# One 512-column matmul for two of 256 in the FFN's first product

## The chip, the core and the metric

The kernel runs on one core of a Trainium2 chip. The metric is the time of one execution in microseconds (us), and of several executions the median. Engines are named as the profile names them: PE is the matmul engine and PEld its weight loads, DVE the vector engine, ACT the scalar engine, POOL the GpSimd engine, SP the engine that issues most transfers. In a matmul the stationary operand is a weight load of 128x128 numbers, and the moving operand is streamed past it, 256 or 512 columns at a time.

## The reference, cut to what matters

A decoder block on 256 tokens of 2048 channels in fp32: two kinds of attention, a merge, and then the part that is changed, a gated MLP with a causal convolution of three taps. `D_FF` is 5632.

```python
    h2 = rmsnorm(x, ffn_norm_w[l])
    up = causal_dwconv(h2 @ w_ffn_up[l], conv_w[l], conv_b[l])
    a, b = jnp.split(up, 2, axis=-1)
    x = x + (jax.nn.silu(a) * b) @ w_ffn_down[l]
return rmsnorm(x, final_norm_w)
```

## The kernel before

All weights of the block are streamed once, in the order of use, in halves of a megabyte (128 partitions of 1024 numbers, 512 KB). Each number is split into a high and a low part that the matmul engine takes exactly (`split2`): ACT copies the high part (`whi`, L129), DVE subtracts it from the number (`wlo`, L130). The activations are split in the same way (`xh`, `xl` for the second norm's output). A product is then three matmuls: high by high, high by low, low by high; low by low is left out. `mm3` records these three.

The work goes in slots, one for each megabyte of weights, 252 in all. In a slot the kernel splits the two halves of the next slot (`part`), lets each task of the postprocessing take one stage (`run_tasks`), and then issues this slot's products (`products`, `issue`). All engines take their instructions in the order of the code. There are four buffers of a split half (`PART_BUFS`), so ACT can start on a half when PE has finished the half that lay there four halves earlier.

A group is 512 columns of one weight matrix. The FFN's first product (kind `up`) has 22 groups of four slots, n = 0, 2, .. 42. A group holds four blocks of 128 columns: of channel blocks n and n+1 the part that becomes `a` and the part that becomes `b`. Its weights are stationary and the 256 tokens move, so a slot is four row tiles by four blocks by three matmuls of 256 columns, 48 matmuls, and a group is 192. The four blocks accumulate in the two PSUM banks of `acc`, two blocks in a bank; `acc` has two buffers, four banks. The other four banks belong to small tiles of the attention and of transposes (`att`).

After a group, two tasks `ffn` run beside the next group's products, the second two slots later, each in four stages: the scaled product into `u` (DVE, L469), the convolution in `y` (ACT L474, DVE L477), the gate `g` (ACT L481, DVE L482), and the split of `g` (ACT L129, DVE L130). The last part of the kernel (kind `dn`) has the weights moving in 512 columns and the activations stationary.

Of the kernel before, what the change touches and what calls it, by code (L numbers as in the profile page):

```python
# [29 lines left out]

# columns of the table of per-channel vectors
V_ATTN, V_RET, V_FFN, V_CONV = 0, 16, 24, 40
# [5 lines left out]
def pieces_in():  # L38
    """Column pieces of w_in, in the order in which the kernel uses them."""
    rw, mw = RH * RD, MH * MD  # L40
    rq, rk, rv, rg = 0, rw, 2 * rw, 3 * rw
    mq = 4 * rw
    mk, mv = mq + mw, mq + 2 * mw
    gr = mq + 3 * mw
    gm = gr + D
    out = []
    for hg in range(2):
        out.append(("mv", hg, [(mv + CW * hg, CW)]))
        for hp in range(2):
            h = 4 * hg + 2 * hp  # L50
            out.append(("mqk", h, [(b + MD * x, MD) for x in (h, h + 1) for b in (mk, mq)]))
    for hg in range(2):
        out.append(("rv", hg, [(rv + CW * hg, CW)]))
        out.append(("rg", hg, [(rg + CW * hg, CW)]))
        for h in (2 * hg, 2 * hg + 1):
            out.append(("rqk", h, [(rk + RD * h, RD), (rq + RD * h, RD)]))
    gates = [(("gr", c, [(gr + CW * c, CW)]), ("gm", c, [(gm + CW * c, CW)])) for c in range(D // CW)]
    return out, gates


def plan():
    """Groups of 512 columns: (what, which, weight, columns, rows)."""
    first, gates = pieces_in()
    groups = [(k, n, "w_in", cols, D) for k, n, cols in first]
    for c in range(D // CW):
        for k, n, cols in gates[c]:
            groups.append((k, n, "w_in", cols, D))
        groups.append(("um", c, "w_moba_up", [(CW * c, CW)], MH * MD))
        groups.append(("ur", c, "w_ret_up", [(CW * c, CW)], RH * RD))
    for c in range(D // CW):  # L70
        groups.append(("wo", c, "w_out", [(CW * c, CW)], D))
    for f in range(0, NFB, 2):
        cols = [(b + P * x, P) for x in (f, f + 1) for b in (0, DFF)]
        groups.append(("up", f, "w_ffn_up", cols, D))
    for c in range(D // CW):
        groups.append(("dn", c, "w_ffn_down", [(CW * c, CW)], DFF))
    return groups
# [3 lines left out]
def block(ctx: ExitStack, tc: tile.TileContext, a):  # L81
# [4 lines left out]
    wp = ctx.enter_context(tc.tile_pool(name="wp", bufs=1))  # L86
    ps = ctx.enter_context(tc.tile_pool(name="ps", bufs=1, space=PSUM))
    px = ctx.enter_context(tc.tile_pool(name="px", bufs=1))
    left, right = ExitStack(), ExitStack()
# [7 lines left out]

# [1 line left out]
    raws, parts = {}, {}  # L99
# [14 lines left out]
    def part(n, *some):  # L114
        """Split a half of a megabyte and send for the one that takes its place."""
        if n < n_halves:
            if n not in parts:
                parts[n] = [wp.tile([P, 2 * CW], F32R, name=x, bufs=PART_BUFS) for x in ("whi", "wlo")]
            for w in some or spans(n):
                split2(parts[n][0][:, w], parts[n][1][:, w], raws[n][:, w])  # L120
            if not some or some[0] == spans(n)[-1]:
                raws.pop(n)
                load(n + RAW_BUFS)

# [1 line left out]
    def split2(hi, lo, full, scale=None):  # L126
        """hi + lo = full (times a number by partition), each exact in fp32r."""
        if scale is None:
            nc.scalar.activation(hi, full, AF.Copy)  # L129
            nc.vector.tensor_sub(lo, full, f32(hi))  # L130
        else:
            nc.scalar.activation(hi, full, AF.Copy, scale=scale)  # L132
            nc.vector.scalar_tensor_tensor(lo, full, scale, f32(hi), op0=OP.mult, op1=OP.subtract)  # L133
# [14 lines left out]
    def issue():  # L148
        """The products of the stream; after a third of them, the others in between."""
        n, m = len(stream), len(between)  # L150
        first, done = n // 3, 0
        for i, one_mm in enumerate(stream):
            one_mm()
            while done < m and done * (n - first) < (i + 1 - first) * m:
                between[done]()
                done += 1
        assert done == m
        stream.clear()
        between.clear()

    def att(name):
        return ps.tile([P, 512], F32, name=name, tag="att", bufs=4)

# [6 lines left out]
    def rsqrt(name, ss, n):  # L170
        """(ss / n + EPS) ** -0.5 by token."""
        nt = ss.shape[1]
        ms = sb.tile([P, nt], F32, name=name + "ms", bufs=2)
        nc.vector.tensor_scalar(ms, ss, 1.0 / n, EPS, op0=OP.mult, op1=OP.add)
        r = sb.tile([P, nt], F32, name=name, bufs=2)
        nc.gpsimd.tensor_tensor(r, ms, mhalf[:, :nt], op=OP.pow)
        return r

    def across(r):
        """[P, NT] by token to [P, S], the same in each partition."""  # L180
        t = att("across")
# [3 lines left out]

# [1 line left out]
    tasks = []  # L187
# [23 lines left out]
    nc.gpsimd.memset(mhalf, -0.5)  # L211
    xh = px.tile([P, KD, S], F32R, name="xh")
    xl = px.tile([P, KD, S], F32R, name="xl")
    ot = {k: px.tile([P, 8, S], F32R, name="ot" + k) for k in ("rh", "rl", "mh", "ml")}
# [38 lines left out]
    def setup():  # L253
        """Constants and the first norm."""
        yield
# [43 lines left out]
    def moba(acc, h, vh, vl):  # L299
        """One head from its keys and queries, [d, (k q) tokens] in PSUM."""  # L300
        hv = slice((h % 4) * MD, (h % 4 + 1) * MD)
# [47 lines left out]
    def retention(acc, h, vh, vl, gate):  # L349
        """One head from its keys and queries, [d, (half tokens)] in a bank each."""  # L350
        hv = slice((h % 2) * RD, (h % 2 + 1) * RD)
# [54 lines left out]
    def flipped(full, dsth, dstl, k0, weight):  # L406
        """[tokens, 512] to hi and lo of its transpose, [channel, k0 .., tokens]."""
        trs = []
# [48 lines left out]
    def ffn_slot(f):  # L457
        """Where the FFN's activations of a block lie, hi and lo."""
        if f < 8:
# [5 lines left out]
    def ffn(acc, f):  # L465
        """A pair of blocks, [channel, (a b) tokens] in PSUM."""
        pf = big["pf"]
        u = big["u"][f % 2]
        nc.vector.tensor_mul(u[:, :, 2:], pair(acc), twice(big["r2b"]))  # L469
        yield  # L470
        y = pf.tile([P, 2, S], F32, name="y", bufs=2)
        cv = [vec[:, V_CONV + 4 * (f + j * NFB):V_CONV + 4 * (f + j * NFB) + 4] for j in range(2)]
# [22 lines left out]
    def finish(acc, t):  # L495
        """The last columns of a tile of tokens, its norm and its way out."""
        c = D // CW - 1
# [16 lines left out]

# [1 line left out]
    now = {}  # L516

    def opened(kind, n):
        """The activations that a group's weights meet: hi and lo, [channel, k, tokens]."""
        if kind in ("mv", "rv"):  # L520
# [27 lines left out]

    def closed(kind, n, acc):
        if kind in ("mv", "rv"):  # L550
# [27 lines left out]
        elif kind == "up":  # L578
            if n == 0:
# [5 lines left out]
                for u in big["u"]:  # L585
                    nc.vector.memset(u[:, :, 0:2], 0.0)
            spawn(ffn, acc[:, 0, :], n)
            spawn(ffn, acc[:, 1, :], n + 1, after=2)
        elif kind == "dn" and n < D // CW - 1:
# [15 lines left out]
    def products(kind, act, accs, kc, halves, tokens, nk):  # L605
        """A megabyte of weights (four tiles of rows) with the activations."""
        for h, (hi, lo) in enumerate(halves):
            for j in range(2):
                kt = 4 * kc + 2 * h + j
                begin, end = kt == 0, kt == nk - 1  # L610
                xs = ffn_slot(kt) if kind == "dn" else [x[:, kt, :] for x in act]
                if kind in ("mqk", "rqk", "up"):
                    for b in range(4):
# [11 lines left out]
    for kind, n, _, _, rows in groups:  # L625
        nk = rows // P
        act = opened(kind, n)
        acc = ps.tile([P, 2, 512], F32, name="acc", bufs=2)
        accs = [acc[:, t, :] for t in range(NT)]
        if (kind, n) == groups[-1][:2]:  # L630
            accs[1] = att("acc1")
        for kc in range(nk // 4):
# [16 lines left out]
            slot += 1  # L649
        closed(kind, n, acc)  # L650
    assert not tasks and not between
    right.close()
    left.close()


# [1 line left out]
def stream(inputs):  # L657
    """The weights in the order of use, in tiles of 256 rows by 512 columns: [n, 128, 1024]."""
    out = []
# [7 lines left out]
def constants():  # L667
    """Angles, decays and masks: what depends on shapes alone."""
    f = np.float32
# [53 lines left out]
```

## Time and profile before

| what | value |
|---|---|
| time, median of 3 runs | 1470.79 us (1470.59 to 1471.25) |
| span of the profiled execution, first to last instruction | 1469.1 us |
| median less span | 1.7 us |
| granted PE clock, mean over the span | 0.997 |
| PE busy | 1455.8 us, 99% of the span |
| products of `up`, first to last | 712.4 to 1220.6 us |
| groups n = 2 to 42 of `up` | 736.73 to 1220.57 us |

The profiled execution has no time of its own beside its span; what a run's time holds around the span is taken as the difference of the two, 1.7 us. Busy shares of PE are not enough to read a matmul stage by, because the recorded matmuls overlap each other: one of 256 columns is recorded with 0.28 us, and the next begins 0.12 us after it. The distance from start to start is what one costs.

### The profile page before, as it was taken

The numbers are of one execution on the slowest core, as the hardware profiler recorded it, in microseconds if no ns is written. First come the engines' busy times: TensorE is split into PE (matmuls) and PEld (weight loads), VectorE is DVE, ScalarE is ACT, GpSimd is POOL, SyncE is SP. The second block draws the span as 40 slices with busy tenths as digits, with TensorE's granted clock in tenths as the row PEclk, the third lists the DMA queues.
The fourth block names the chain that finished last, engine by engine and source line by source line (L and its number), as shares of the span: only waits on it lengthen the run. The fifth ranks groups of instructions, "written<-read, shape, count | busy, mean of one in ns | idle before, by whom it ended". The sixth has DMA issues, their size and how long they took to land.

```text
span 1469.1 us, 22790 instructions
## 1 busy us (share of the span) xinstructions
PE 1455.8 (99%) x9254; PEld 1319.4 (90%) x9254; DVE 869.7 (59%) x1072; ACT 687.4 (47%) x891; POOL 58.8 (4%) x45
## 2 busy tenths in 40 slices
PE   8999999999999999999999999999999999999997
PEld 6989889899888888888999999999999998888886
DVE  7665755656454545555566666666666666545453
ACT  6444453444444444445455545554455445344343
POOL 2120200101000000000000000000000000000000
PEclk9999999999999999999999999999999999999999
DMA  8544445554455555556555555555555555555553
GB/s 282 199 170 168 163 169 176 173 186 173 173 185 198 190 188 191 209 200 214 173 187 183 182 181 186 184 179 184 186 186 180 180 187 215 199 189 198 189 198 116
DMA packets 77849, 274.35 MB, mean 187 GB/s; under 512 B 8720, under 2 KB 9776, under 8 KB 77616
## 3 DMA queue, kind: packets, MB, share of 16 engines
q1 hardware_dynamic: 77024, 271.84, 53.4%
q8 instruction: 72, 1.18, 0.3%
q10 hardware_dynamic: 720, 1.06, 0.2%
q14 instruction: 33, 0.27, 0.0%
HBM read 270.77 MB, written 2.10 MB: 186 GB/s over the span
## 4 chain that ended last, share of the span: by engine, by line
PE 97%; DMA 1%; issue 1%; ACT 1%; DVE 0%; SPq 0%; POOLq 0%; POOL 0%; ACTq 0%; DVEq 0%
PE acc L138 95%; DMA xt<-in_xT 1%; PE ftr L146 0%; PE s L138 0%; PE o L138 0%; PE rs L138 0%; PE ro L138 0%; ACT xh L132 0%; PE pt L146 0%; DVE xl L133 0%; PE tr L146 0%; DVE wlo L130 0%; ACT sqk L248 0%; ACT x L509 0%; POOLq L719 0%
## 5 line engine op out<-in xcount | busy, mean ns | idle before, releaser
L130 DVE TENSOR_TENSOR wlo<-raw,whi 128x1024 fp32r<-128x1024 f32 (+1 forms) x506 | 626.1, 1238 | 567.8 <-ACT whi L129 566.9
L129 ACT ACTIVATE whi<-raw 128x1024 fp32r<-128x1024 f32 (+1 forms) x506 | 534.1, 1056 | 736.4 <-PE acc L138 603.3
L138 PE MATMUL acc<-xh,wlo 128*128 128x256 f32 x1920 | 545.1, 284 | 0.0
L138 PE MATMUL acc<-xh,whi 128*128 128x256 f32 x1920 | 544.6, 284 | 0.0
L138 PE MATMUL acc<-xl,whi 128*128 128x256 f32 x1920 | 544.2, 283 | 0.0
L138 PEld LDWEIGHTS acc<-xh,whi 128*128 128x128 f32 x1920 | 368.3, 192 | 0.1
L138 PEld LDWEIGHTS acc<-xl,whi 128*128 128x128 f32 x1920 | 368.3, 192 | 0.2
L138 PEld LDWEIGHTS acc<-xh,wlo 128*128 128x128 f32 x1920 | 368.3, 192 | 0.0
L138 PE MATMUL acc<-wlo,xh 128*128 128x512 f32 x448 | 178.2, 398 | 2.4 <-DVE wlo L130 2.4
L138 PE MATMUL acc<-whi,xh 128*128 128x512 f32 x448 | 178.6, 399 | 0.7 <-ACT whi L129 0.7
L138 PE MATMUL acc<-whi,xl 128*128 128x512 f32 x448 | 178.3, 398 | 0.0
L138 PEld LDWEIGHTS acc<-wlo,xh 128*128 128x128 f32 x448 | 84.7, 189 | 20.9 <-DVE wlo L130 4.2
L138 PEld LDWEIGHTS acc<-whi,xh 128*128 128x128 f32 x448 | 84.7, 189 | 18.4 <-ACT whi L129 1.8
L138 PEld LDWEIGHTS acc<-whi,xl 128*128 128x128 f32 x448 | 84.7, 189 | 17.1
L138 PE MATMUL acc<-whi,gh 128*128 128x512 f32 x224 | 87.1, 389 | 0.0
L138 PE MATMUL acc<-wlo,gh 128*128 128x512 f32 x224 | 87.1, 389 | 0.0
L138 PE MATMUL acc<-whi,gl 128*128 128x512 f32 x224 | 87.1, 389 | 0.0
L477 DVE SCALAR_TENSOR_TENSOR y<-u,vec,y 128x256 f32<-128x256 f32 x176 | 73.4, 479 | 0.0
L138 PE MATMUL acc<-whi,mgh 128*128 128x512 f32 x128 | 50.9, 398 | 0.0
L138 PE MATMUL acc<-whi,mgl 128*128 128x512 f32 x128 | 50.9, 397 | 0.0
L138 PE MATMUL acc<-wlo,mgh 128*128 128x512 f32 x128 | 50.6, 395 | 0.0
L138 PE MATMUL acc<-whi,otmh 128*128 128x512 f32 x128 | 50.0, 391 | 0.0
(158 smaller groups left out, 1174.9 us busy)
## 6 DMA issues: line engine op xcount, KB each, us to landing
raw<-in_wts SPq DMA_DIRECT2D x502, 512.0 KB, 3.4
xp<-in_x SPq DMA_DIRECT2D x4, 512.0 KB, 5.5
xt<-in_xT SPq DMA_DIRECT2D x7, 256.0 KB, 5.6
raw<-in_wts SPq DMA_DIRECT2D x4, 256.0 KB, 4.1
wf<-in_wf SPq DMA_DIRECT2D x1, 1024.0 KB, 5.6
out<-x SPq DMA_DIRECT2D x4, 256.0 KB, 2.9
out<-x ACTq DMA_DIRECT2D x4, 256.0 KB, 3.0
decay<-in_decay SPq DMA_DIRECT2D x1, 512.0 KB, 4.6
```

Of the source, the lines that this page charges most:

```text
L129: nc.scalar.activation(hi, full, AF.Copy)
L130: nc.vector.tensor_sub(lo, full, f32(hi))
L138: to.append(lambda: nc.tensor.matmul(out, a, b, **kw))
L477: nc.vector.scalar_tensor_tensor(y[:, j, :], u[:, j, i:i + S], cv[j][:, i:i + 1], y[:, j, :], op0=OP.mult, op1=OP.add)
```

## The change

In the groups n = 2 to 42 of `up` (21 of the 22), the high part of a weight block meets the high and the low part of the activations in one matmul of 512 columns instead of two of 256. For that the two parts of the activations lie side by side in one tile `xb`, of which `xh` and `xl` are now views. Each block then fills a whole PSUM bank: the left 256 columns collect high by high and low by high, the right 256 collect high by low. So a group has four banks, `acc` and a new `acc2` (`second_pair`), with two buffers each: all eight. The four banks of `att` are closed before the first such group. `ffn` adds the two halves of the bank: ACT copies the right halves to `y`, DVE adds the left halves, and DVE scales the sum into `u`; before, DVE scaled from PSUM in one step. The last group's second accumulator comes from `acc2` and not from `att`.

```diff
+    banks = ExitStack()
+    spare = {"att": banks.enter_context(tc.tile_pool(name="psa", bufs=1, space=PSUM))}
...
+    def second_pair():
+        if "up" not in spare:
+            banks.close()
+            spare.pop("att")
+            spare["up"] = banks.enter_context(tc.tile_pool(name="psu", bufs=1, space=PSUM))
+        return spare["up"].tile([P, 2, 512], F32, name="acc2", bufs=2)
...
-    xh = px.tile([P, KD, S], F32R, name="xh")
-    xl = px.tile([P, KD, S], F32R, name="xl")
+    xb = px.tile([P, KD, 2, S], F32R, name="xb")
+    xh, xl = xb[:, :, 0, :], xb[:, :, 1, :]
...
-        nc.vector.tensor_mul(u[:, :, 2:], pair(acc), twice(big["r2b"]))
-        yield
         y = pf.tile([P, 2, S], F32, name="y", bufs=2)
+        if len(acc.shape) == 2:
+            full = pair(acc)
+        else:
+            full = y
+            nc.scalar.activation(y, acc[:, :, S:], AF.Copy)
+            nc.vector.tensor_add(y, acc[:, :, :S], y)
+        nc.vector.tensor_mul(u[:, :, 2:], full, twice(big["r2b"]))
+        yield
...
-                if kind in ("mqk", "rqk", "up"):
+                if len(accs) == 4:
+                    for b in range(4):
+                        w = slice(j * CW + b * P, j * CW + (b + 1) * P)
+                        mm(accs[b], hi[:, w], xb[:, kt, :, :], start=begin, stop=False, to=stream)
+                        mm(accs[b][:, :S], lo[:, w], xs[0], start=False, stop=end, to=stream)
+                elif kind in ("mqk", "rqk", "up"):
...
+        more = None
+        if kind == "up" and n >= 2:
+            more = second_pair()
+            accs += [more[:, t, :] for t in range(NT)]
```

On PE, where the group n = 2 begins, the program before has these rows (a row is out<-moving,stationary and partitions x columns; the numbers are buffers):

```order
L138 MATMUL acc_6225<-xh_76,wlo_6372 128x256
L138 MATMUL acc_6508<-xh_76,whi_6436 128x256
L138 MATMUL acc_6508<-xl_77,whi_6436 128x256
L138 MATMUL acc_6508<-xh_76,wlo_6437 128x256
L138 MATMUL acc_6508<-xh_76,whi_6436 128x256
```

The changed program has at the same place:

```order
L140 MATMUL acc_6227<-xb_79,wlo_6374 128x256
L140 MATMUL acc_6510<-xb_79,whi_6438 128x512
L140 MATMUL acc_6510<-xb_79,wlo_6439 128x256
L140 MATMUL acc_6510<-xb_79,whi_6438 128x512
L140 MATMUL acc_6510<-xb_79,wlo_6439 128x256
L140 MATMUL acc2_6515<-xb_79,whi_6438 128x512
L140 MATMUL acc2_6515<-xb_79,wlo_6439 128x256
```

Three matmuls of a block have become two, of 512 and 256 columns in turn, with nothing between them.

On DVE, in the slot after a group in which the first of its `ffn` tasks takes its first stage, the rows before are (names in brackets are the engines and queues whose semaphores an instruction waits for):

```order
L130 TENSOR_TENSOR wlo_7045<-raw_6914,whi_7044 128x1024 [waits DMAHW3_49,PE_49,Activation_49]
L482 TENSOR_TENSOR g_7050<-g_7050,y_6982 128x256 [waits DVE_49,Activation_49]
L469 TENSOR_TENSOR u0_6504<-acc_6770,r2b_6448 128x2x256
L130 TENSOR_TENSOR wlo_7103<-raw_6972,whi_7102 128x1024 [waits DMAHW4_49,PE_49,Activation_49]
L130 TENSOR_TENSOR wlo_7109<-raw_6978,whi_7108 128x1024 [waits DMAHW5_49,PE_49,Activation_49]
```

And after the change:

```order
L132 TENSOR_TENSOR wlo_6930<-raw_6828,whi_6929 128x1024 [waits DMAHW3_49,PE_49,Activation_49]
L499 TENSOR_TENSOR g_6935<-g_6935,y_6833 128x256 [waits DVE_49,Activation_49]
L486 TENSOR_TENSOR y_6938<-acc_6713,y_6938 128x512 [waits Activation_49]
L487 TENSOR_TENSOR u0_6506<-y_6938,r2b_6450 128x2x256 [waits DVE_49]
L132 TENSOR_TENSOR wlo_6975<-raw_6873,whi_6974 128x1024 [waits DMAHW4_49,PE_49,Activation_49]
L132 TENSOR_TENSOR wlo_6981<-raw_6879,whi_6980 128x1024 [waits DMAHW5_49,PE_49,Activation_49]
```

One addition stands ahead of the scaling and waits for ACT; the scaling reads `y` and no longer PSUM. ACT's copy of the right halves stands in the same slot behind that slot's second `whi` and the gate's `g`.

## Rows read from the trace of the kernel before

**Rows 1.** The page: busy time by engine, and the chain that ended last, by engine.

```profile
PE 1455.8 (99%) x9254; PEld 1319.4 (90%) x9254; DVE 869.7 (59%) x1072; ACT 687.4 (47%) x891; POOL 58.8 (4%) x45
PE 97%; DMA 1%; issue 1%; ACT 1%; DVE 0%; SPq 0%; POOLq 0%; POOL 0%; ACTq 0%; DVEq 0%
```

**Rows 2.** Busy time by window: one up group, all 21, and part of dn.

```profile
core 0: us, PE busy (x) PEld busy (x) DVE busy (x) ACT busy (x) POOL busy (x), PEclk, DMA share, GB/s
736.73:759.77 23.04, 23.04 (x194) 23.04 (x193) 14.84 (x20) 12.46 (x15) 0.00 (x0) 1.00 0.52 183
736.73:1220.57 483.84, 483.84 (x4034) 483.84 (x4033) 321.56 (x460) 246.00 (x335) 0.00 (x0) 1.00 0.53 184
1230.00:1440.00 210.00, 210.00 (x928) 173.88 (x927) 105.85 (x95) 88.01 (x96) 0.00 (x0) 1.00 0.56 194
```

**Rows 3.** Timeline of PE in up and at its end: start, duration, instruction.

```profile
759.77 0.28 PE L138 MATMUL acc<-xh,whi 128*128 128x256 f32 x1
759.89 0.28 PE L138 MATMUL acc<-xl,whi 128*128 128x256 f32 x1
...
1220.45 0.28 PE L138 MATMUL acc<-xh,wlo 128*128 128x256 f32 x1
1220.57 0.40 PE L138 MATMUL acc<-whi,otrh 128*128 128x512 f32 x1
...
1221.73 0.39 PE L138 MATMUL acc<-whi,otrl 128*128 128x512 f32 x1
```

**Rows 4.** Timeline of PE inside dn, first and last of 55 matmuls.

```profile
1299.71 0.39 PE L138 MATMUL acc<-wlo,otmh 128*128 128x512 f32 x1
...
1311.95 0.39 PE L138 MATMUL acc<-wlo,gh 128*128 128x512 f32 x1
```

**Rows 5.** Timeline of PE in a gate group with retention's matmuls in between.

```profile
270.58 0.39 PE L138 MATMUL acc<-whi,xl 128*128 128x512 f32 x1
270.81 0.28 PE L138 MATMUL rs<-rh 128*128 128x256 f32 x1
270.92 0.40 PE L138 MATMUL acc<-whi,xh 128*128 128x512 f32 x1
271.15 0.28 PE L138 MATMUL rs<-rl,rh 128*128 128x256 f32 x1
271.27 0.40 PE L138 MATMUL acc<-wlo,xh 128*128 128x512 f32 x1
271.51 0.28 PE L138 MATMUL rs<-rh,rl 128*128 128x256 f32 x1
271.63 0.40 PE L138 MATMUL acc<-whi,xl 128*128 128x512 f32 x1
```

**Rows 6.** Timeline of ACT in a slot of up; in brackets idle before, and releaser.

```profile
852.06 1.06 ACT L129 ACTIVATE whi<-raw 128x1024 fp32r<-128x1024 f32 x1 [1.82 <-PE acc L138]
853.03 0.40 ACT L481 ACTIVATE g<-y 128x256 f32<-128x256 f32 x1
854.94 1.06 ACT L129 ACTIVATE whi<-raw 128x1024 fp32r<-128x1024 f32 x1 [1.52 <-issue]
```

**Rows 7.** Timeline of DVE: the norm's copy, then the same slot of up.

```profile
733.29 0.42 DVE L455 COPY r2b<-across 128x256 f32<-128x256 f32 x1
...
853.15 1.23 DVE L130 TENSOR_TENSOR wlo<-raw,whi 128x1024 fp32r<-128x1024 f32 x1 [1.48 <-ACT whi L129]
854.30 0.42 DVE L482 TENSOR_TENSOR g<-g,y 128x256 f32<-128x256 f32 x1
854.63 0.68 DVE L469 TENSOR_TENSOR u<-acc,r2b 128x512 f32<-128x512 f32 x1
856.04 1.23 DVE L130 TENSOR_TENSOR wlo<-raw,whi 128x1024 fp32r<-128x1024 f32 x1 [0.72 <-ACT whi L129]
```

**Rows 8.** Groups of instructions: count, busy us, mean ns, idle before.

```profile
L130 DVE TENSOR_TENSOR ml<-mfull,mh 128x512 fp32r<-128x512 f32 x8 | 5.5, 684 | 0.0
L130 DVE TENSOR_TENSOR mgl<-ftr,mgh 128x512 fp32r<-128x512 f32 x8 | 5.1, 682 | 0.0
L129 ACT ACTIVATE mgh<-ftr 128x512 fp32r<-128x512 f32 x8 | 4.3, 585 | 0.0
```

More of the change, by code (lines that the diff above doesn't have):

```diff
@@ L161, in att @@
     def att(name):
-        return ps.tile([P, 512], F32, name=name, tag="att", bufs=4)
+        return spare["att"].tile([P, 512], F32, name=name, tag="att", bufs=4)
+    def second_pair():
[4 more added lines that the diff above has]
+        return spare["up"].tile([P, 2, 512], F32, name="acc2", bufs=2)
     def pair(ap):
@@ L468, in ffn @@
         u = big["u"][f % 2]
-        nc.vector.tensor_mul(u[:, :, 2:], pair(acc), twice(big["r2b"]))
+        y = pf.tile([P, 2, S], F32, name="y", bufs=2)
+        if len(acc.shape) == 2:
[5 more added lines that the diff above has]
+        nc.vector.tensor_mul(u[:, :, 2:], full, twice(big["r2b"]))
         yield
-        y = pf.tile([P, 2, S], F32, name="y", bufs=2)
         cv = [vec[:, V_CONV + 4 * (f + j * NFB):V_CONV + 4 * (f + j * NFB) + 4] for j in range(2)]
@@ L547, in opened, with closed @@
         return xh, xl
-    def closed(kind, n, acc):
+    def closed(kind, n, acc, more):
         if kind in ("mv", "rv"):
@@ L586, in closed @@
                     nc.vector.memset(u[:, :, 0:2], 0.0)
-            spawn(ffn, acc[:, 0, :], n)
-            spawn(ffn, acc[:, 1, :], n + 1, after=2)
+            pairs = [acc[:, 0, :], acc[:, 1, :]] if more is None else [acc, more]
+            spawn(ffn, pairs[0], n)
+            spawn(ffn, pairs[1], n + 1, after=2)
         elif kind == "dn" and n < D // CW - 1:
@@ L629, in block @@
         accs = [acc[:, t, :] for t in range(NT)]
+        more = None
+        if kind == "up" and n >= 2:
+            more = second_pair()
+            accs += [more[:, t, :] for t in range(NT)]
         if (kind, n) == groups[-1][:2]:
-            accs[1] = att("acc1")
+            accs[1] = second_pair()[:, 0, :]
         for kc in range(nk // 4):
@@ L649, in block @@
             slot += 1
-        closed(kind, n, acc)
+        closed(kind, n, acc, more)
     assert not tasks and not between
@@ L653, in block @@
     left.close()
+    banks.close()
 def stream(inputs):
```

## The prediction

> **What bounds the kernel now.** I read the chain that ended last first: PE holds 97% of it, and PE is busy for 99% of the span [rows 1]. The kernel is as long as its matmuls, so the question is what a matmul costs in the stage that is changed, and whether PE is ever kept waiting there.
>
> The windows answer the second part. From 736.73 to 1220.57 us, the 21 groups that the change touches, PE is busy for all of 483.84 us, DVE for 321.56 and ACT for 246.00, with the full clock granted [rows 2]. PE waits for nothing. The others wait for PE: ACT's `whi` at 852.06 was released by the end of a product [rows 6], that is, by a buffer of split weights coming free.
>
> For the first part the recorded durations are of no use: a matmul of 256 columns is recorded with 0.28 us, but the next starts 0.12 us later [rows 3]. So I go from start to start. The window holds 21 x 192 = 4032 products, and 483.84 / 4032 = 0.1200 us for each; the timeline shows the same distance from its first row to its last [rows 2, 3]. In the last stage, where matmuls have 512 columns, 54 distances take 1311.95 - 1299.71 = 12.24 us, 0.2267 us each [rows 4]. A straight line through the two is 13.3 ns for a matmul, plus 0.4167 ns for a column. That is 2.4 GHz, the upper of the two clock levels, at one column a cycle. The same columns in half as many matmuls therefore cost 2 x 120.0 - 226.7 = 13.3 ns less. I draw two points only, and the line says nothing yet on matmuls of both widths in turn.
>
> **PE's part of the change.** It removes, in each of 21 groups and for each of 64 pairs of row tile and block, two matmuls of 256 columns with a weight load each, and adds one of 512. That is 21 x 64 = 1344 pairs fewer by one matmul and one load. The low part's matmul stays. The columns streamed stay the same. What a block costs per row tile is now 3 x 120.0 = 360.0 ns. By the line it becomes 226.7 + 120.0 = 346.7 ns. The sum is 1344 x 13.33 = 17.9 us.
>
> The weight loads don't stand against this. In up each load has to be done within a matmul of 256 columns, and PEld is busy throughout by its records; in dn, with longer matmuls, it is busy for 173.88 of 210.00 us [rows 2]. After the change the load for the low part has a matmul of 512 columns to hide behind, and that for the next high part has one of 256, which is what every load in up has now.
>
> What the trace of before lacks is a long steady run of 512 and 256 in turn. It has short ones. In a gate group retention's matmuls of 256 columns fall between the stream's of 512: three pairs take 0.34, 0.35 and 0.36 us [rows 5], on average 0.350. And the first five matmuls of 512 that follow up take 1.16 us, 0.232 each, before they settle at 0.227 [rows 3]. So a matmul next to one of another width can cost some ns more than the line says, and once less. Bounds for a pair are then 340 ns from below (a saving of 1344 x 20 = 26.9 us) and 360 ns from above (no saving). I take the line's 346.7. It lies inside these bounds, and where the widths repeat regularly this trace settles within a few matmuls to distances that fall on it; the rows of the short runs are all taken from a stretch that has not settled, with other tiles and tasks in between.
>
> The Trainium skill would make the gain smaller: "TensorE: Matmul & The Clock Gate", section Back-to-back issue gap, gives N / 2.4 + 2.5 ns for the distance of warm matmuls, so a fixed part of 2.5 ns each. By that figure the sum would be 1344 x 2.5 = 3.4 us, and the time an estimated 1467.4 us. The trace has the same slope and 13.3 ns in place of 2.5, so the measurement decides; a case in which most of the fixed part stays is among the rivals.
>
> **The other engines' part.** For each of 42 pairs of blocks ACT gets one copy of 128x512 from PSUM and DVE one addition of 128x512; the scaling stays, but reads SBUF in place of PSUM. Nearest rows: the copy `mgh` from PSUM takes 585 ns, a DVE operation with one operand in PSUM 682, one with both in SBUF 684 [rows 8]. So DVE gets 42 x 0.682 = 28.6 us more, ACT 42 x 0.585 = 24.6 us. Per group DVE goes from 14.84 us to 16.2, ACT from 12.46 to 13.6, while a group shrinks from 23.04 to 64 x 0.3467 = 22.19 us [rows 2]. Neither becomes the longer one.
>
> I cost them at nothing, and the work that hides them is PE's. In the slot where an `ffn` task takes its first stage, DVE scales until 855.31 and then stands idle until 856.04, waiting for the `whi` that begins at 854.94 [rows 6, 7]. The added 0.68 us nearly fills this gap. On ACT the copy falls into the 1.52 us ahead of that `whi`. What is queued behind the waiting addition is the scaling and the next slot's `wlo`, and PE waits for the latter. But that is far ahead: the `wlo` that ends at 854.38 belongs to a half whose buffer came free at 852.06, and with four buffers three halves of 24 x 0.12 = 2.88 us lie before its use, at about 860.7. It is some 6 us early. If this cover were gone, the price would be at most the whole 28.6 us.
>
> Two waits are new in principle. The first use of `acc2` has to wait until the `att` banks are read out. The last reader is the copy of `r2b` at 733.29 [rows 7]; the first matmul that needs them stands four matmuls behind the group's start at 736.73, over 3 us later. And all eight banks are taken, in two sets. Each set is read in the first slot (`acc`) and in the third slot (`acc2`) of the next group, and is written again one group later, so one to three slots of 5.5 us are left. Both I cost at nothing.
>
> The stream of weights runs 4% faster in this stage, from a DMA share of 0.53 [rows 2]; nothing there is near a limit. The transfers are issued behind the `wlo` as before.
>
> **Sum.** 1469.1 - 17.9 = 1451.2 us of span. The median of the runs is 1.7 us above the span, which gives 1452.9 us, 1.2% less than 1470.79.
>
> **Rivals.**
>
> The pairs don't settle. Matmuls of two widths in turn go on as in the short runs, with 350 ns a pair: 1344 x 10 = 13.4 us, 1457.4 us. At 355 ns it would be 6.7 us, 1464.1 us. For it speak that these are the only rows of such turns and that the 512s behind up need five matmuls to settle; against it, that every regular stretch of this trace does settle. Near the far end, at 357 ns, nearly all of the fixed part stays with the pair: a saving of 1344 x 3 = 4.0 us, 1466.8 us; 2% of the case's chance is for that. It is also about what the page's formula comes to. At about 357.8 ns a pair the gain would be lost in what a measurement of this kernel can tell, 0.2% or 2.9 us.
>
> The pair is cheaper than the line. The first pair of the short run takes 0.34 us [rows 5]. If a matmul of 256 behind one of 512 always took 113 ns, as there, because its load is long done, the time would be 1443.9 us. Against it: the load of the next 512 must still be done within the 256, and in up that costs 120.
>
> It gets slower. In the short run each pair is 10 ns longer than the one ahead of it. If that went one step beyond the last, to 370 ns, the stage would lose 1344 x 10 = 13.4 us, 1484.2 us. It decides from 362 ns. For it speaks only that row's trend; against it, that a distance that grows without end has no cause in the profile, since both loads have as much room as now or more.
>
> **How the numbers follow.** The line 52%, pairs that don't settle 32% (3% of it too small a gain to measure, another 1% between that and no gain), cheaper pairs 9%, slower 7%, in which I count a wait of PE for DVE that I have overlooked. The likeliest gives 1452.9 us, by itself 1451 to 1455. The range goes from the cheap bound, 1444, to pairs of 355 ns, 1464; that leaves out the end of the second case and the slower ones, somewhat under 2 in 10, since the rows on alternating widths are few. Faster by over 0.2%: 52 + 28 + 9, so 0.89; within 0.2%: 0.04; slower: 0.07.
>
> **What would show it.** In the changed kernel's timeline of PE the distance from a 512 to the 256 behind it should be 0.227 us and from there to the next 512 0.120, and a group should take 22.19 us. The 21 groups should take 466 us, with PE busy for all of it, the added operations should take 0.58 and 0.68 us, and the waits of ACT and DVE should still be for PE and for each other. Distances of 0.230 to 0.240 behind each 256 would show the second case; gaps of PE ahead of a `wlo` would show that DVE's cover was thinner than I read; a gap once, where the first `acc2` is written, would show the wait for the `att` banks. I am wrong above all if the cost of a matmul depends on the width of its neighbours.

## The result, and the profile after

The changed kernel takes 1462.59 us, against 1470.84 us for the kernel before in the same measurements: a ratio of 0.9944, 95% interval 0.993 to 0.9957. One of its four runs, with a granted clock of 0.654, took 2039.31 us; the ratio goes by the other three. The changed kernel is faster by 8.2 us. I had said 17.9 us, 1452.9 us in all, with a range up to 1464. The time lies within the range, but the gain is less than half of the one forecast.

The page of the changed kernel has these two rows (busy time by engine; the chain that ended last):

```profile
PE 1446.5 (99%) x7910; PEld 1246.1 (85%) x7910; DVE 896.4 (61%) x1114; ACT 707.9 (48%) x933; POOL 58.9 (4%) x45
PE 97%; issue 1%; DVE 1%; DMA 1%; SPq 0%; ACT 0%; POOLq 0%; POOL 0%; ACTq 0%; DVEq 0%
```

PE is still the chain, as in [rows 1], with 9254 - 7910 = 1344 matmuls fewer, as counted. The windows of the changed stage (a group, then all 21):

```profile
core 0: us, PE busy (x) PEld busy (x) DVE busy (x) ACT busy (x) POOL busy (x), PEclk, DMA share, GB/s
737.19:759.80 22.61, 22.61 (x130) 19.60 (x129) 14.84 (x20) 12.46 (x15) 0.00 (x0) 1.00 0.58 188
737.19:1212.07 474.88, 474.88 (x2690) 411.73 (x2689) 346.86 (x500) 265.48 (x375) 0.00 (x0) 1.00 0.58 187
```

The stage went from 483.84 us [rows 2] to 474.88, which is 8.96 us less; the rest of the span, 986 us, is 0.7 us longer. The place where this stage starts moves about by that much in the traces of this study (736.20 to 737.69 us), so nothing is to be read into it. Within the stage PE is busy for the whole window, and the clock is the full one. So no wait has eaten the gain. The matmuls themselves take longer than I said: 474.88 us / 1344 = 353.3 ns a pair, not 346.7. The timeline of PE shows how (start, duration, instruction):

```profile
780.30 0.40 PE L140 MATMUL acc<-xb,whi 128*128 128x512 f32 x1
780.54 0.28 PE L140 MATMUL acc<-xb,wlo 128*128 128x256 f32 x1
780.65 0.40 PE L140 MATMUL acc<-xb,whi 128*128 128x512 f32 x1
780.88 0.28 PE L140 MATMUL acc<-xb,wlo 128*128 128x256 f32 x1
781.00 0.40 PE L140 MATMUL acc<-xb,whi 128*128 128x512 f32 x1
781.24 0.28 PE L140 MATMUL acc<-xb,wlo 128*128 128x256 f32 x1
781.36 0.40 PE L140 MATMUL acc<-xb,whi 128*128 128x512 f32 x1
```

Three pairs take 1.06 us, and then the same pattern begins again: a 512 holds PE for 0.24, 0.23, 0.24 us, a 256 for 0.11 or 0.12. It is regular, but it is not the regularity that I expected: 512s of 0.230 to 0.240 us behind each 256 were the prediction's sign of its second case. By the trace's start times, which are whole nanoseconds, the pairs of the cycle are 236 + 113, 232 + 118 and 241 + 120 ns. And this had been there before: the second and third pair of [rows 5] are 232 + 118 and 241 + 120 ns, with other tiles and other banks.

The added operations, in the groups of instructions of this stage (count, busy us, mean ns, idle before):

```profile
L487 DVE TENSOR_TENSOR u<-y,r2b 128x512 f32<-128x512 f32 x40 | 27.7, 692 | 1.4
L486 DVE TENSOR_TENSOR y<-acc,y 128x512 f32<-128x512 f32 x40 | 27.4, 684 | 0.0
L485 ACT ACTIVATE y<-acc 128x512 f32<-128x512 f32 x40 | 23.1, 578 | 0.0
```

And DVE's timeline in a slot in which an `ffn` task takes its first stage:

```profile
851.48 1.23 DVE L132 TENSOR_TENSOR wlo<-raw,whi 128x1024 fp32r<-128x1024 f32 x1 [1.38 <-ACT whi L131]
852.63 0.42 DVE L499 TENSOR_TENSOR g<-g,y 128x256 f32<-128x256 f32 x1
852.96 0.68 DVE L486 TENSOR_TENSOR y<-acc,y 128x512 f32<-128x512 f32 x1
853.68 0.69 DVE L487 TENSOR_TENSOR u<-y,r2b 128x512 f32<-128x512 f32 x1
854.30 1.23 DVE L132 TENSOR_TENSOR wlo<-raw,whi 128x1024 fp32r<-128x1024 f32 x1
```

The idle 0.72 us ahead of the second `wlo` in [rows 7] is filled by the addition, and `wlo` begins without a gap. Ahead of the first `wlo` DVE still waits 1.38 us for ACT's `whi`.

### The profile page after: what moved, and what is told of

Same layout as the page of the kernel before. It is cut to its first block, busy times and chain, and to the rows that moved or that the text cites. A ratio compares the mean times of both kernels' runs of the same rounds, so it can differ in the third digit from the quotient of the medians.

```text
span 1460.8 us, 20167 instructions
## 1 busy us (share of the span) xinstructions
PE 1446.5 (99%) x7910; PEld 1246.1 (85%) x7910; DVE 896.4 (61%) x1114; ACT 707.9 (48%) x933; POOL 58.9 (4%) x45
## 3 DMA queue, kind: packets, MB, share of 16 engines
q10 hardware_dynamic: 720, 1.06, 0.2%
## 4 chain that ended last, share of the span: by engine, by line
PE 97%; issue 1%; DVE 1%; DMA 1%; SPq 0%; ACT 0%; POOLq 0%; POOL 0%; ACTq 0%; DVEq 0%
PE acc L140 95%; DMA raw<-in_wts 1%; PE ftr L148 0%; PE s L140 0%; DVE xb L135 0%; PE o L140 0%; PE rs L140 0%; PE ro L140 0%; DVE wlo L132 0%; PE pt L148 0%; SPq L114 0%; PE tr L148 0%; SPq L237 0%; ACT x L526 0%; POOLq L747 0%
## 5 line engine op out<-in xcount | busy, mean ns | idle before, releaser
L140 PE MATMUL acc<-xb,whi 128*128 128x512 f32 (+1 forms) x2496 | 689.7, 346 | 0.0
L140 PE MATMUL acc<-xb,wlo 128*128 128x256 f32 x1920 | 542.2, 282 | 0.0
L140 PEld LDWEIGHTS acc<-xb,whi 128*128 128x128 f32 x2496 | 433.9, 190 | 63.4
L140 PEld LDWEIGHTS acc<-xb,wlo 128*128 128x128 f32 x1920 | 364.2, 190 | 0.0
L140 PE MATMUL acc<-whi,xb 128*128 128x512 f32 x896 | 289.5, 397 | 0.7 <-ACT whi L131 0.7
L140 PEld LDWEIGHTS acc<-whi,xb 128*128 128x128 f32 x896 | 164.6, 188 | 35.0 <-ACT whi L131 1.8
L140 PE MATMUL acc<-wlo,xb 128*128 128x512 f32 x448 | 178.0, 397 | 3.3 <-DVE wlo L132 3.3
L140 PEld LDWEIGHTS acc<-wlo,xb 128*128 128x128 f32 x448 | 84.3, 188 | 22.9 <-DVE wlo L132 6.5
L140 PE MATMUL acc<-whi,otml 128*128 128x512 f32 x128 | 49.9, 390 | 0.0
L140 PE MATMUL acc<-wlo,otmh 128*128 128x512 f32 x128 | 49.9, 390 | 0.0
```

The costliest lines, as they stand in the source:

```text
L140: to.append(lambda: nc.tensor.matmul(out, a, b, **kw))
```

## The experiments

The theory after the result: matmuls of one width, repeated, cost 13.3 ns + 0.4167 ns a column, and each change of width disturbs that rhythm for some matmuls, so strict turns never reach it. The first rival: the cost lies in what else the change brings, the new layout, a bank for each block, the added reads of PSUM. The experiments keep everything of the changed kernel but the order or the widths of the matmuls in the 21 groups.

**tile4: four 512s, then four 256s.**

```diff
                     for b in range(4):
                         w = slice(j * CW + b * P, j * CW + (b + 1) * P)
                         mm(accs[b], hi[:, w], xb[:, kt, :, :], start=begin, stop=False, to=stream)
+                    for b in range(4):
+                        w = slice(j * CW + b * P, j * CW + (b + 1) * P)
                         mm(accs[b][:, :S], lo[:, w], xs[0], start=False, stop=end, to=stream)
```

> The changed kernel, but within a row tile the four matmuls of 512 columns come first and then the four of 256, so the width changes twice per eight matmuls and not with each one. Theory (a 512 behind a 256 is slow until the rhythm settles; the row where up gave way to dn has 233, 236, 228, 233 ns for the first four, 23 ns too much in all, and a 256 behind a 512 is 7 ns short): 346.7 + (23 - 7) / 4 = 350.8 ns a pair, 1462.6 - 1344 x 0.0025 = about 1459.2 us, and that pattern in the timeline. Rival (the cost is in the layout, the 512 columns in one bank, or the change of bank with each block): still 353.3 ns a pair or more, since now each matmul changes the bank, 1462.6 us or over.

Measured: 1459.08 us, ratio to the kernel before 0.9921 (0.9906 to 0.9936). The window of the 21 groups:

```profile
737.49:1209.00 471.51, 471.51 (x2690) 412.03 (x2689) 346.04 (x500) 265.61 (x376) 0.00 (x0) 1.00 0.56 188
```

471.51 / 1344 = 350.8 ns a pair, the number of the theory (its pattern is looked at below, with run8). Now every matmul goes to another bank than the one ahead of it, twice as many changes of bank as in the changed kernel, and it is faster: banks are not the cost.

**slot16 and snake32: runs of 16 and of 32.** In slot16 the loops over the two halves, the row tiles and the blocks stand inside one over high and low; in snake32 every other slot has the low parts first.

```diff
+        if len(accs) == 4:
+            for low in (False, True):            # snake32: (kc % 2 == 1, kc % 2 == 0)
+                for i in range(4):
+                    kt = 4 * kc + i
+                    for b in range(4):
+                        w = slice(i % 2 * CW + b * P, i % 2 * CW + (b + 1) * P)
+                        if low:
+                            mm(accs[b][:, :S], halves[i // 2][1][:, w], xb[:, kt, 0, :], ...
+                        else:
+                            mm(accs[b], halves[i // 2][0][:, w], xb[:, kt, :, :], ...
+            return
```

> The same with all sixteen matmuls of 512 columns of a slot first and then its sixteen of 256. Theory: the transient of five matmuls, 28 ns, less 7 ns, once in sixteen pairs: 348.0 ns a pair, 1462.6 - 1344 x 0.0053 = about 1455.4 us. Rival (layout or banks): 353.3 ns and 1462.6 us. Rival (the splitting comes late because all low parts are used at the end and their buffers come free later): gaps of PE ahead of a slot, and a time over 1456 us by as much.

> As slot16, but every other slot has the 256s first, so that runs of 32 of one width follow each other and the width changes half as often. Theory: 347.3 ns a pair, about 1454.5 us, some 0.9 us under slot16. Rival (layout or banks): 1462.6 us. Rival (late splitting): more than slot16, since low parts are wanted at the start of a slot.

Measured: slot16 1455.03 us, ratio 0.9894 (0.9878 to 0.9911); snake32 1454.31 us, 0.9889 (0.9874 to 0.9903). Their windows, slot16 first:

```profile
736.64:1204.24 467.60, 467.60 (x2690) 413.28 (x2689) 345.00 (x500) 269.31 (x377) 0.00 (x0) 1.00 0.58 189
```

```profile
736.96:1203.75 466.79, 466.79 (x2691) 413.45 (x2689) 348.35 (x500) 263.77 (x375) 0.00 (x0) 1.00 0.58 190
```

That is 347.9 and 347.3 ns a pair. PE has no gap, so the later use of the low parts did not make the splitting late. The same matmuls, in another order, are 8 us faster than in the changed kernel: snake32 beats both kernels and is 1.4 us above what I had predicted for the changed one. That the cost is in the order is shown by this; layout, banks and postprocessing are the same in all.

**all256: the widths of before in the new layout.**

```diff
-                        mm(accs[b], hi[:, w], xb[:, kt, :, :], start=begin, stop=False, to=stream)
+                        mm(accs[b][:, :S], hi[:, w], xs[0], start=begin, stop=False, ...
+                        mm(accs[b][:, S:], hi[:, w], xs[1], start=False, stop=False, ...
```

> The changed layout, the four banks a group and the longer postprocessing stay, but the high part meets the two parts of the activations in two matmuls of 256 columns again (left half and right half of the bank). Theory: 120.0 ns for each matmul, 360 ns a block and row tile, 1462.6 + 1344 x 0.0067 = about 1471.5 us, level with the kernel before. Rival (layout, banks, or ACT and DVE reading PSUM slow PE down): distances over 120 ns, or gaps, and 1475 us or more.

Measured: 1470.63 us, ratio 0.9999 (0.999 to 1.0009). The window:

```profile
736.20:1220.04 483.84, 483.84 (x4034) 483.84 (x4033) 348.89 (x500) 265.37 (x375) 0.00 (x0) 1.00 0.53 184
```

483.84 us to the hundredth, as in [rows 2], although DVE has 27 us more to do. So the added work of ACT and DVE, `xb` and the eight banks cost nothing, as predicted, and the first rival is gone.

**run2 and run8: other lengths.** run2 takes blocks two by two, high, high, low, low; run8 does a half's eight high parts and then its eight low parts.

> Runs of two: two 512s, two 256s. Theory (each 512 behind a 256 starts the transient 233, 236, 228, 233, 231 ns; a 256 behind a 512 is 7 ns short): 346.7 + (16 - 7) / 2 = 351.2 ns a pair, 1462.6 - 1344 x 0.0021 = about 1459.8 us, between tile4 and the changed kernel. Rival (a fixed cost for each change of width, 3.3 ns): 346.7 + 3.3 = 350.0 ns, 1458.1 us.

> Runs of eight: the eight matmuls of 512 columns of a half, then its eight of 256. By the transient seen in slot16 (28 ns on five 512s behind a 256, 7 ns short on the first 256 behind a 512): 346.7 + 21 / 8 = 349.3 ns a pair, 1462.6 - 1344 x 0.0040 = about 1457.2 us. If runs of an even length settle as run2 did: 348 ns, 1455.5 us.

Measured: run2 1455.77 us, ratio 0.9898 (0.9882 to 0.9915); run8 1457.18 us, 0.9909 (0.9893 to 0.9926). Their windows, run2 first:

```profile
737.49:1205.65 468.16, 468.16 (x2691) 408.48 (x2689) 345.64 (x500) 265.73 (x375) 0.00 (x0) 1.00 0.57 190
```

```profile
737.19:1206.47 469.28, 469.28 (x2690) 412.98 (x2689) 345.63 (x500) 266.27 (x376) 0.00 (x0) 1.00 0.56 190
```

run8 has 349.2 ns a pair, the transient's number. run2 has 348.3, less than tile4 and about a nanosecond less than run8 and less than either theory said. Its timeline (merged rows, two matmuls in each):

```profile
780.45 0.40 PE L140 MATMUL acc<-xb,wlo 128*128 128x256 f32 x2
780.68 0.63 PE L140 MATMUL acc<-xb,whi 128*128 128x512 f32 x2
781.15 0.39 PE L140 MATMUL acc<-xb,wlo 128*128 128x256 f32 x2
781.38 0.62 PE L140 MATMUL acc<-xb,whi 128*128 128x512 f32 x2
781.84 0.40 PE L140 MATMUL acc<-xb,wlo 128*128 128x256 f32 x2
```

Here two 256s take 0.23 us, less than the 0.24 that they take in a long run, and two 512s 0.46 to 0.47, more than 0.453. So the transient (the first 512s behind a 256 take longer than 226.7 ns, the first 256 behind a 512 is short), as read from the entry to a long run, is too dear for runs of two: a matmul's cost depends on more than one neighbour.

The start times in the traces show how far the transient holds. Averaged over the window by the place in the run, the 512s of run8 take 233.3, 235.8, 228.3, 232.5 and 230.9 ns and from the sixth on 226.7; the 256s take 113.3 and 119.2 ns, and from the third on 120.0. slot16 and snake32 have the same. In tile4 only the sums are the theory's: four 512s take 929 ns (theory 930), four 256s 474 (473), but the first 256 takes 117.5 ns in place of 113. That tile4's mean came out to the tenth is in part luck.

**alt384, all512, all384: which changes of width cost.** Each was timed once, so they are read by their windows, at a granted clock of 1.00. The low part's matmul, or both, get other widths, with the products added or left out as the expectations say. In all384 the high part's matmul gets the same 384 columns as the low part's, in all row tiles but a group's first.

```diff
-                        mm(accs[b][:, :S], lo[:, w], xs[0], start=False, stop=end, to=stream)
+                        mm(accs[b][:, :384], lo[:, w], xb[:, kt, :, :].rearrange("p a s -> p (a s)")[:, :384], ...   # alt384
+                        mm(accs[b], lo[:, w], xb[:, kt, :, :], ...                                # all512
```

> The changed kernel's strict turns, but the low part meets 384 columns instead of 256 (the high part of the activations and half of their low part, a product that is otherwise left out), so that a 512 alternates with a 384. By the line 13.3 ns + 0.4167 ns a column a pair would be 226.7 + 173.3 = 400.0 ns. Theory A (the rhythm is lost because the next weight load only just fits under a matmul of 256 columns): with 384 there is room, 400.0 ns a pair, steady, 1462.6 + 1344 x 0.0467 = about 1525 us. Theory B (any change of width loses it): 406 ns or more a pair, about 1533 us or over, distances that move about.

> The low part meets both parts of the activations too (it adds low by low, which is otherwise left out), so every matmul of the changed groups has 512 columns, the load of a low part still alternating with that of a high part. Theory (only the width counts): 226.7 ns for each, 453.3 ns a pair, steady, 1462.6 + 1344 x 0.1 = about 1597 us. Rival (streaming xb, the four banks or turns of high and low weights cost something): over 226.7 ns, each 3 ns of it 8 us more.

> High and low part both meet 384 columns (the last 128 of high by low are left out except in a group's first row tile, and half of low by low is added), so that the width no longer changes. If a change of width is what costs in alt384: 13.3 + 384 x 0.4167 = 173.3 ns for each matmul, steady, and 346.7 ns a pair, by chance the same as the line gave for 512 and 256; the first row tile's four pairs of each group, 512 and 384 in turn, add 4 x 21 x 0.067 = 6 us: about 1459 us. Rival (384 columns are an unfavourable width by themselves): 180 ns or so and 1477 us.

Measured: alt384 1542.93 us, all512 1596.74 us, all384 1459.75 us. Their windows, in this order:

```profile
736.86:1292.37 555.51, 555.51 (x2691) 488.96 (x2690) 352.82 (x500) 265.61 (x375) 0.00 (x0) 1.00 0.48 161
```

```profile
736.90:1346.21 609.31, 609.31 (x2690) 504.52 (x2689) 352.93 (x500) 265.50 (x375) 0.00 (x0) 1.00 0.44 147
```

```profile
737.69:1209.20 471.51, 471.51 (x2690) 467.53 (x2689) 347.42 (x500) 265.48 (x375) 0.00 (x0) 1.00 0.56 188
```

all512 has 609.31 / 2688 = 226.7 ns for each matmul: with high and low weights in turn, `xb` as moving operand and four banks, but one width, the distance is that of [rows 4]. all384, less the 84 pairs of its first row tiles at alt384's price, has (471.51 - 84 x 0.4133) / 1260 = 346.7 ns for two matmuls, 173.3 each: 384 columns lie on the line too. And alt384, made of these two widths in turn, has 413.3 ns a pair where the line gives 400.0. Its timeline:

```profile
780.25 0.40 PE L140 MATMUL acc<-xb,whi 128*128 128x512 f32 x1
780.49 0.34 PE L140 MATMUL acc<-xb,wlo 128*128 128x384 f32 x1
780.66 0.40 PE L140 MATMUL acc<-xb,whi 128*128 128x512 f32 x1
780.90 0.34 PE L140 MATMUL acc<-xb,wlo 128*128 128x384 f32 x1
```

It is steady from pair to pair, and steadily 13.3 ns too long, more than the 6.7 ns of 512 and 256. A theory that I had held possible falls with it: that turns cost because the load for the next 512 only just fits under a matmul of 256. Under 384 columns it has 53 ns more room, and the turns cost more. (The records say nothing on this room: a load is recorded with 187 to 192 ns in all these traces, more than a 256 or a 384 takes from start to start, also where the widths don't change and nothing is lost.)

The start times show where the loss lies. Averaged over the windows, a 512 in strict turns takes 236.3 ns beside 256s and 237.5 beside 384s, 10 to 11 ns over the line in both. The 256 takes 117.0 ns, 3 under the line, and the 384 takes 175.9, 2.6 over it. So the 512s pay nearly the same in both kinds of turns, and the narrower matmul makes the difference.

The prices of a pair, less the line's, from the windows:

| kernel | equal widths in a row | ns a pair | over the line, ns |
|---|---|---|---|
| changed kernel | 1 | 353.3 | 6.7 |
| run2 | 2 | 348.3 | 1.7 |
| tile4 | 4 | 350.8 | 4.2 |
| run8 | 8 | 349.2 | 2.5 |
| slot16 | 16 | 347.9 | 1.3 |
| snake32 | 32 | 347.3 | 0.6 |
| alt384 (512 and 384) | 1 | 413.3 | 13.3 |

## Why the prediction was right and wrong

**Right: what bounds the stage, and the line.** PE alone set the time, before and after. The line of 13.3 ns and 0.4167 ns a column, drawn through two widths, holds at a third (all384) and for runs of one width in the new layout (all256, all512). The Trainium skill's formula for the gap of warm matmuls ("TensorE: Matmul & The Clock Gate", Back-to-back issue gap), which that section gives for an isolated matmul, has 2.5 ns for the fixed part; at the three widths measured here, with a weight load for each matmul, it is 13.3 ns.

**Right: the work that was costed at nothing.** The added operations took 578, 684 and 692 ns where the rows of other operations had said 585, 682 and 684, and DVE's idle gap took them up. all256 shows the price of all of it together: none that can be measured. The hand-over of the `att` banks cost nothing either: PE has no gap in the window that holds it.

**Wrong: the cost of a pair.** The step that failed is the one in which I took the line's 346.7 ns for a 512 and a 256 in turn, and set aside [rows 5], whose three pairs average 350, as a stretch that had not settled. What I had seen was that runs of one width settle on the line within some five matmuls. I carried that over to turns, where nothing in the trace showed it. The turns did settle, but on a cycle of three pairs with 1.06 us, 353.3 ns each. The term was mis-sized by 6.7 ns of 13.3: half the gain. The time still lies in the range only because the range was drawn to the second case's 355 ns a pair.

The rows had almost the number. Of the three pairs of [rows 5] the first, 0.34 us, is the entry from a run of 512s; the second and third, 0.35 and 0.36, are two pairs of the cycle. Leaving the entry out would have given 355 ns. My second case, pairs that don't settle, had the price (350 to 355 ns) and the sign, and was half right on the mechanism: the neighbour's width does raise the cost, but the pairs do settle, above the line. It had 32% against 52% for the line, by an argument on what regular stretches do and not by the one row that had the shape of the changed code.

**Open.** Why a change of width costs at all. It is not the bank, the operands, the order of high and low weights, or the other engines. It is not the stream of weights either, whose DMA share is 0.58 in the changed kernel as in slot16 and snake32, and more room for a weight load did not lower it (alt384). No run shows what in PE sets the price, no view of the profile here goes inside a matmul, and the price does not fall steadily with the length of a run (run2 against tile4).

## What to carry to other kernels

Merging two matmuls that share their weights saves the fixed part of one, here 13.3 ns, but only to the extent that the widths don't then alternate: put the matmuls of one width together. Here runs of 16 and 32 came within 1.3 and 0.6 ns a pair of the line; among the short runs the order has to be measured, since runs of two were cheaper than runs of four or eight. When a change brings a pattern that the trace has only in a few rows, let these rows set the price, and take the entry into the pattern out of their mean.

## What the runs showed of the hardware that was not expected

Matmuls with a new weight load each follow each other by 13.3 ns + 0.4167 ns a column at 256, 384 and 512 columns (120.0, 173.3, 226.7 ns), as long as the width stays. Strict turns of 512 and 256 settle on a cycle of three pairs, 353.3 ns each; of 512 and 384 on one of 413.3 ns, 13.3 ns over the line. Turns of two and two of 512 and 256 cost a quarter of what strict turns do: 1.7 against 6.7 ns a pair. In runs of eight and more, the first five 512s behind a 256 take 27 to 28 ns more than the line in all, and the first two 256s behind a 512 take 7 to 8 ns less.
